# One more run of Strassen quads in the second half of each output projection

## The chip, the core and the metric

The kernel runs on one core of one Trainium2 chip. Five engines work in parallel, each through its own list of instructions in order: TensorE (PE in the profile, with its weight loads as PEld), VectorE (DVE), ScalarE (ACT), GpSimd (POOL) and SyncE (SP), which here only issues transfers. They wait for one another by semaphores. The metric is the device time of one execution in microseconds; lower is better. The kernel before takes 2047.71 us, the median of three runs that lie between 2047.55 and 2047.89.

## What is computed

A decoder trunk of two layers on 256 tokens of width 2048, all in float32. Layer 0 attends over one block, layer 1 over a window of 128 with shared keys and values; behind each attention stand an output projection, a residual with layer norm, a gated feed-forward net with a causal convolution of width 3, and a second residual with layer norm. Cut to the place that matters:

```python
h = x
for layer in range(2):
    attn = attention(h) @ w_o[layer]              # (256 x 2048) @ (2048 x 2048)
    h = layer_norm(ALPHA * h + attn, ln_g[layer, 0], ln_b[layer, 0])
    ffn = conv_ffn(h, w_up[layer], conv_w[layer], conv_b[layer], w_down[layer])
    h = layer_norm(ALPHA * h + ffn, ln_g[layer, 1], ln_b[layer, 1])
```

The change is in the two products with `w_o`.

## The kernel before, in words

**Numbers in two parts.** A float32 value is held as a high part in the fast format fp32r and a low part, the rest, in the same format. A product of two such matrices is three matmuls: high by high, high by low, low by high. `mm` and `product` issue these three (L497 to L499 for `product`). The high part of a weight tile is written by ACT (L168, `wh<-raw`), the low part by DVE (L177, `wl<-raw,wh`); `raw` is the tile as it was loaded.

**Halves.** Weights stream in as halves: tiles of 128 x 1024 float32, 512 KB, two blocks of 128 x 512 each. `load_weights` issues a load on SP as soon as the split of an older half frees one of 6 raw buffers; `split_upto` splits halves some places ahead of the one that PE takes. The split halves live in 4 buffers (`spool`), so that a split normally waits until PE has finished the half four places earlier. Near the end of a projection, `settle` gives some halves homes in tiles that are free by then (`xT`, the coming stage's `up`), and the table `reach` lets the splits run up to 9 halves ahead there.

**The output projection** (`project_out` with `PLAN_O`). Rows of the weight are 16 blocks of 128 (k), columns 4 chunks of 512 (n); the chunks are worked in two pairs, (0, 1) and (2, 3). A plain block (k, n) is multiplied with both groups of 128 tokens: two products, so a plain half is four. A quad is two rows k by the two chunks of a pair, by the two token groups: 8 products if plain, 7 by Strassen's scheme. `_mixed` writes the order: groups of plain halves, between them runs of two quads, each run 7 halves with two products each (`SEVEN`). Two of the seven halves (named T1,T3 and T2,T4) hold sums of weight blocks, which `presums` has made earlier on DVE (L444) and stored in DRAM; the sums of the token side are made by `sums` for each run, into xT, ahead of its first summed half.

**Banks.** A projection's partial results live in PSUM: four banks named acc, one for each chunk of a pair and group of tokens, and four named at, shared with the attention and the transposes. In a chunk pair with quads, the four at banks hold the shared products P1, P5, P7 and P6 through all runs of that pair. When the last run of the pair is over, `fold` adds them into the residual: three steps, put at the following three halves by `at`, of DVE instructions L513, L514, L518 (sums of the banks) and L612 or L614 (`into`: adds into `res`, the residual; the first time it also scales it by ALPHA; the last time L618 takes the statistics of the layer norm). `evac` does the same for an acc bank when its last product is done. A bank can be written anew when the last instruction that reads it has run.

**Order of the work.** The order on each engine is that in which the program issues its instructions (`manual_schedule`). `take` issues, for each half, the splits ahead and whatever `at` has put there; `step` counts the halves. Before: the first pair has 5 plain halves, 7 of a run, 3 plain, 7 of a run; the second pair 16 plain halves, the last 8 of which are the window, worked for the first group of tokens and then for the second, so that the layer norm of the first group runs under the second. 38 halves in all. In the window, `late` issues evacuations, the norm (L636, L637) and the transposes for the next stage (L670 on PE, from `res`).

Of the kernel before, what the change touches and what calls it, by code (L numbers as in the profile page):

```python
# [21 lines left out]
KB = D // P  # L22
NH = 16
# [4 lines left out]
NCH = D // 512  # L28
# [19 lines left out]
NQ = 12  # L48
PLAINS = ((5, 2, 2, 2, 2, 0, 6), (0, 1, 1, 1, 1, 0, 15))
NQ_O = 4  # L50
PLAINS_O = (5, 3, 0)
IN_PARTS = (True, False)
NV = 2 * 8 + 4 * 8
SEVEN = (("B11", "B21"), ("T1", "T3"), ("T2", "T4"), ("B22", "B22"), ("B11", "B21"), ("T1", "T3"), ("T2", "T4"))
# [10 lines left out]
def _mixed(c, groups, plain, p0):  # L65

    plan, at = [], 0
    for i, g in enumerate(groups):
        plan += plain[at:at + g]
        at += g  # L70
        if i < len(groups) - 1:
            plan += [tuple((b, p0 + 2 * i + p, c) for b, p in zip(bs, ps)) for bs, ps in zip(SEVEN, PAIR_OF)]
    assert at == len(plain)
    return plan


PLAN_O = _mixed(0, PLAINS_O, _plain(range(NH - 2 * NQ_O), (0, 1)), NH // 2 - NQ_O) + _plain(range(NH), (2, 3))
PLAN_V = _mixed(1, PLAINS_O, _plain(range(KB - 2 * NQ_O), (2, 3)), KB // 2 - NQ_O)
PLAN_DOWN = [h for c in range(2) for h in _mixed(c, PLAINS[c], _plain(range(2 * NQ, FT), (2 * c, 2 * c + 1)), 0)]
QUADS = {}  # L80
for _l in range(2):
    QUADS[2 * _l] = [(2 * _l, 0, NH // 2 - NQ_O + p) for p in range(NQ_O)]
    QUADS[2 * _l + 1] = [(2 * _l + 1, c, p) for c in range(2) for p in range(NQ)]
QUADS[4] = [(4, 1, KB // 2 - NQ_O + p) for p in range(NQ_O)]
ORDER = [q for li in (4, 0, 1, 2, 3) for q in QUADS[li]]
AHEAD_OF = {0: QUADS[4] + QUADS[0] + QUADS[1][:2], 1: QUADS[1][2:], 2: QUADS[2], 3: QUADS[3]}


def _summed(half):
# [17 lines left out]
def trunk(ctx: ExitStack, tc: tile.TileContext, wst, wsum, xT_in, x_in, relb, onehot, umask, sinks, conv_in, ln_g, ln_b, out):  # L107
# [449 lines left out]
    def project_out(src, plan, li, homes, preload, turnover=None, quad_blocks=None):  # L557
# [135 lines left out]

        def late(t, i):
            last = i == WINDOW - 1
            if t == 0 and last:
                evac(NCH - 1, 0)
                sd = moments(0)
                nc.vector.reciprocal(rs[0], sd)
                for c in COLS[0]:  # L700
                    norm(0, c)
            if t == 1 and after:
                if 3 <= i < 7:
                    c = COLS[0][i - 3]
                    low(0, c, turn(0, c))
                if 5 <= i < 7:
                    high_upto(n0 + i + 1)
            if t == 1 and last:
                evac(NCH - 1, 1)
                if after:  # L710
                    sd = moments(1)
                    nc.vector.reciprocal(rs[1], sd)
                else:
                    last_norm()
            if t == 1 and not after and 2 <= i < NCH + 1:
                scaled_ahead(i - 2)

        if quads:
            groups = PLAINS[0] if ns == 3 else PLAINS_O
            for i in range(len(groups) - 1):  # L720
                m = 4 if i and not groups[i] else sum(groups[:i]) + 7 * i - (ns == 3) if i else ns == 3
                for j, f in enumerate(sums(i)):
                    at(m + j, f)
        evacuated, folded = set(), set()
# [111 lines left out]
    def layer_attention(l, rest, stage, turnover):  # L836
# [65 lines left out]
        def v_pair():  # L902
            src = lambda k: xT[:, k, :]
            k0 = KB - 2 * NQ_O
            vts, begun = {}, set()

            def place(i):
                flat = st[:, NH // 2 + 4 * i:NH // 2 + 4 * i + 4, :].rearrange("p a b -> p (a b)")
                return flat.rearrange("p (h q s c) -> p h q s c", h=2, q=2, s=4)

            def into(t, n, a):
                if n not in vts:
                    vts[n] = pool.tile([P, 2, 512], F32, name="vt", bufs=2)
                d = vts[n][:, t, :]
                if (t, n) in begun:
                    nc.vector.tensor_tensor(out=d, in0=d, in1=a, op=ALU.add)
                else:
                    begun.add((t, n))
                    nc.scalar.activation(d, a, AF.Copy)

            parted = mixed(src, PLAN_V, k0 // 2, 4, lambda i: xT[:, k0 + 4 * i:k0 + 4 * i + 4, :], place, into)
            mv = Moving(src, 0)
            for i in range(len(PLAINS_O) - 1):
                for j, f in enumerate(parted.sums(i)):
                    at(sum(PLAINS_O[:i]) + 7 * i + j, f)
            evacuated = set()
            for half in PLAN_V:
                blocks = [mv.block() for _ in range(2)]
                for e, w in zip(half, blocks):
                    for tgt in parted.target(e):  # L930
                        parted.product(*tgt, *w)
                step()
                for n in (2, 3):
                    for t in range(2):
                        if (n, t) not in evacuated and parted.done((n, t)):
                            evacuated.add((n, t))
                            at(0, lambda n=n, t=t: into(t, n, parted.banks.pop((n, t))))
            parted.fold(1)
            run(before)
            return {n: in_parts(4 + i, v, "vt", 512, 2) for i, (n, v) in enumerate(sorted(vts.items()))}  # L940
# [280 lines left out]
```

## Time and profile before

| | us |
|---|---|
| median of 3 runs | 2047.71 |
| the profiled execution | 2047.9 |
| its span, first to last instruction | 2045.8 |
| PE busy in the span | 2035.9 |
| DVE busy | 1715.4 |
| ACT busy | 1159.0 |
| projection of layer 0 | about 294 to 385 |
| projection of layer 1 | about 1245 to 1335 |

The granted clock of TensorE is 1.00 over the whole span. The span is what the engines' instructions cover, and about 2 us of the execution lie around it. In a list in order of time, a row has start, duration, engine, line, operation, output<-inputs, and the number of equal instructions that it merges; in brackets stands how long the engine was idle before it and what ended this. A matmul's duration is its way through the array (0.39 us here), and the next starts before it ends, so the cost of a matmul is the distance between two starts.

### The profile page before, as it was taken

The numbers are of one execution on the slowest core, as the hardware profiler recorded it, in microseconds if no ns is written. First come the engines' busy times: TensorE is split into PE (matmuls) and PEld (weight loads), VectorE is DVE, ScalarE is ACT, GpSimd is POOL, SyncE is SP. The second block draws the span as 40 slices with busy tenths as digits, with TensorE's granted clock in tenths as the row PEclk, the third lists the DMA queues.
The fourth block names the chain that finished last, engine by engine and source line by source line (L and its number), as shares of the span: only waits on it lengthen the run. The fifth ranks groups of instructions, "written<-read, shape, count | busy, mean of one in ns | idle before, by whom it ended". The sixth has DMA issues, their size and how long they took to land.

```text
span 2045.8 us, 30050 instructions
## 1 busy us (share of the span) xinstructions
PE 2035.9 (100%) x10940; PEld 1760.4 (86%) x10940; DVE 1715.4 (84%) x2495; ACT 1159.0 (57%) x1737; POOL 79.6 (4%) x146
## 2 busy tenths in 40 slices
PE   9999999999999999999999999999999999999999
PEld 8888888988888888888888888898888888888887
DVE  6778888888888888899896788978888888889887
ACT  5556556455555555566673556545555555566673
POOL 0100000000000000000000000000000000000000
PEclk9999999999999999999999999999999999999999
DMA  8888888478888888889994767838888888879894
GB/s 299 307 293 320 286 297 303 167 249 302 283 296 295 288 295 290 286 282 330 330 364 156 263 214 251 288 126 291 307 300 312 305 300 302 299 265 328 314 357 165
DMA packets 161892, 578.19 MB, mean 283 GB/s; under 512 B 19360, under 2 KB 21728, under 8 KB 160464
## 3 DMA queue, kind: packets, MB, share of 16 engines
q1 hardware_dynamic: 138080, 500.08, 70.8%
q0 software_dynamic: 21312, 73.84, 9.2%
q10 hardware_dynamic: 2352, 2.36, 0.4%
q8 instruction: 86, 1.41, 0.3%
q14 instruction: 62, 0.51, 0.1%
HBM read 511.12 MB, written 69.26 MB: 284 GB/s over the span
## 4 chain that ended last, share of the span: by engine, by line
PE 93%; DVE 4%; issue 1%; DMA 1%; ACT 1%; DVEq 0%; ACTq 0%
PE acc L330 38%; PE acc L332 20%; PE acc L499 6%; PE acc L498 6%; PE acc L497 6%; PE at L498 2%; PE at L499 2%; PE at L497 2%; PE acc L357 1%; DVE wl L177 1%; DMA raw<-in_wst_dram 1%; PE acc L394 1%; PE acc L395 1%; PE acc L393 1%; PE acc L369 1%
## 5 line engine op out<-in xcount | busy, mean ns | idle before, releaser
L177 DVE TENSOR_TENSOR wl<-raw,wh 128x1024 fp32r<-128x1024 f32 (+1 forms) x760 | 905.5, 1220 | 160.7 <-ACT wh L168 138.3
L168 ACT ACTIVATE wh<-raw 128x1024 fp32r<-128x1024 f32 (+1 forms) x760 | 776.7, 1053 | 195.6 <-PE acc L499 113.2
L330 PE MATMUL acc<-xT,wh 128*128 128x512 f32 x3456 | 829.7, 392 | 0.0
L330 PEld LDWEIGHTS acc<-xT,wh 128*128 128x128 f32 x3456 | 642.5, 188 | 127.5
L332 PEld LDWEIGHTS acc<-xT,wl 128*128 128x128 f32 x3456 | 443.4, 190 | 11.9
L332 PE MATMUL acc<-xT,wl 128*128 128x256 f32 x3456 | 451.0, 284 | 0.0
L1035 ACT ACTIVATE h<-acc 128x256 f32<-128x256 f32 x172 | 66.0, 384 | 409.2 <-PE acc L332 203.4
L1043 DVE SCALAR_TENSOR_TENSOR c<-h,cw,c 128x255 f32<-128x255 f32 x344 | 165.4, 481 | 9.1 <-ACT c L1039 2.8
L444 DVE TENSOR_TENSOR gb<-gb 128x512 f32<-128x512 f32 x240 | 164.2, 684 | 0.0
L1036 DVE TENSOR_TENSOR h<-acc,h 128x256 f32<-128x256 f32 x172 | 72.5, 422 | 57.3 <-ACT h L1035 57.0
L448 POOL DMA_DIRECT2D ws<-gb x120 | 64.1, 534 | 1414.1 <-DVE gb L444 1122.1
L497 PE MATMUL acc<-wh,up 128*128 128x512 f32 x275 | 107.1, 390 | 0.0
L498 PE MATMUL acc<-wl,up 128*128 128x512 f32 x275 | 107.1, 390 | 0.0
L499 PE MATMUL acc<-wh,up 128*128 128x512 f32 x275 | 107.1, 389 | 0.0
L1039 ACT ACTIVATE c<-h,cw 128x256 f32<-128x256 f32 x172 | 101.9, 592 | 0.0
L497 PE MATMUL acc<-wh,st 128*128 128x512 f32 x178 | 70.1, 394 | 0.0
L499 PE MATMUL acc<-wh,st 128*128 128x512 f32 x178 | 69.4, 390 | 0.0
L498 PE MATMUL acc<-wl,st 128*128 128x512 f32 x178 | 69.4, 390 | 0.0
L497 PEld LDWEIGHTS acc<-wh,up 128*128 128x128 f32 x275 | 51.7, 188 | 10.7
L498 PEld LDWEIGHTS acc<-wl,up 128*128 128x128 f32 x275 | 51.7, 188 | 10.6
L499 PEld LDWEIGHTS acc<-wh,up 128*128 128x128 f32 x275 | 51.7, 188 | 10.6
L948 ACT ACTIVATE qT<-acc 128x256 f32<-128x256 f32 x32 | 12.3, 384 | 71.5 <-PE acc L332 46.1
(231 smaller groups left out, 2219.1 us busy)
## 6 DMA issues: line engine op xcount, KB each, us to landing
raw<-in_wst_dram SPq DMA_DIRECT2D x692, 512.0 KB, 5.2
gb<-in_wsum_dram SPq DMA_DIRECT2D x120, 512.0 KB, 7.7
ws<-gb POOLq DMA_DIRECT2D x120, 512.0 KB, 5.7
raw<-ws SPq DMA_DIRECT2D x120, 512.0 KB, 5.7
bias<-band POOLq DMA_DIRECT2D x8, 512.0 KB, 8.4
band<-ud POOLq DMA_DIRECT2D x4, 512.0 KB, 12.0
band<-ud ACTq DMA_DIRECT2D x4, 512.0 KB
res<-in_x_dram SPq DMA_DIRECT2D x2, 1024.0 KB, 7.3
```

Source lines behind the costliest of these rows:

```text
L168: nc.scalar.activation(wh[:, c], raws[s][:, c], AF.Copy)
L177: nc.vector.tensor_tensor(out=wl[:, c], in0=raws[s][:, c], in1=wh[:, c].bitcast(F32), op=ALU.subtract)
L330: nc.tensor.matmul(acc, w, xT[:, k, :], start=(k == 0), stop=(k == ends[0]))
L332: nc.tensor.matmul(acc[:, 0:T], w, xT[:, k, 0:T], start=False, stop=(k == ends[1]))
L444: nc.vector.tensor_tensor(out=w[:, o:o + 512], in0=a, in1=b, op=op)
L497: nc.tensor.matmul(acc, sh, wh, start=first, stop=False)
L498: nc.tensor.matmul(acc, sh, wl, start=False, stop=False)
L499: nc.tensor.matmul(acc, sl, wh, start=False, stop=last)
L1035: nc.scalar.activation(h, acc[:, T:2 * T], AF.Copy)
L1036: nc.vector.tensor_tensor(out=h, in0=acc[:, 0:T], in1=h, op=ALU.add)
L1039: nc.scalar.activation(c, h, AF.Identity, bias=w[:, 3:4], scale=w[:, 2:3])
L1043: nc.vector.scalar_tensor_tensor(c[:, d:T], h[:, 0:T - d], w[:, 2 - d:3 - d], c[:, d:T], op0=ALU.mult, op1=ALU.add)
```

## The change

The first chunk pair keeps its two runs, with 4, 2 and 2 plain halves around them where there were 5, 3 and 0. The second pair begins with a run of two quads (rows 12 to 15 of the weight), and 12 plain halves follow. Its token-side sums are those that the second run of the first pair has made already. Per projection 41 halves then stand where there were 38. The sums of weight blocks for these quads are two more per layer: those of layer 0 are made in the first attention stage, in place of two of the down projection's, which move into the feed-forward stage together with layer 1's two. `late` evacuates acc banks that become complete within the window. The last hunk only keeps the value projection, which shared the table, at 5, 3, 0.

```diff
-PLAINS_O = (5, 3, 0)
+PLAINS_O = (4, 2, 2)
+PLAINS_V = (5, 3, 0)
...
-PLAN_O = _mixed(0, PLAINS_O, _plain(range(NH - 2 * NQ_O), (0, 1)), NH // 2 - NQ_O) + _plain(range(NH), (2, 3))
-PLAN_V = _mixed(1, PLAINS_O, _plain(range(KB - 2 * NQ_O), (2, 3)), KB // 2 - NQ_O)
+PLAN_O = _mixed(0, PLAINS_O, _plain(range(NH - 2 * NQ_O), (0, 1)), NH // 2 - NQ_O) + _mixed(
+    1, (0, 12), _plain(range(NH - NQ_O), (2, 3)), NH // 2 - 2)
+PLAN_V = _mixed(1, PLAINS_V, _plain(range(KB - 2 * NQ_O), (2, 3)), KB // 2 - NQ_O)
...
-    QUADS[2 * _l] = [(2 * _l, 0, NH // 2 - NQ_O + p) for p in range(NQ_O)]
+    QUADS[2 * _l] = [(2 * _l, c, NH // 2 - NQ_O + p) for c in range(2) for p in range(2 * c, NQ_O)]
...
-AHEAD_OF = {0: QUADS[4] + QUADS[0] + QUADS[1][:2], 1: QUADS[1][2:], 2: QUADS[2], 3: QUADS[3]}
+AHEAD_OF = {0: QUADS[4] + QUADS[0], 1: QUADS[1] + QUADS[2][:2], 2: QUADS[2][2:], 3: QUADS[3]}
...
         def late(t, i):
             last = i == WINDOW - 1
+            for n in range(NCH - 1):
+                if (n, t) not in evacuated and done((n, t)):
+                    evacuated.add((n, t))
+                    evac(n, t)
...
-                m = 4 if i and not groups[i] else sum(groups[:i]) + 7 * i - (ns == 3) if i else ns == 3
+                m = 4 if i and not groups[i] else sum(groups[:i]) + 7 * i - (groups[i] == 2) if i else ns == 3
```

In the changed kernel all lines of the projection stand a few lines lower (L497 is L499, L612 is L614, L614 is L616, L618 is L620, L177 is L179).

**PE, end of the first chunk pair, layer 0.** Of each product the first of its three matmuls is shown. Before, behind the last run (its last three products are the first three rows), the plain halves of the second pair follow on acc banks:

```order
L497 MATMUL at_3371<-xT_143 128x512
L497 MATMUL at_3381<-xT_143 128x512 [waits Activation_49]
L497 MATMUL acc_3212<-xT_143,st_145 128x512
L497 MATMUL acc_3609<-xT_143,st_145 128x512 [waits Activation_49]
L497 MATMUL acc_3613<-xT_143,st_145 128x512
L497 MATMUL acc_3609<-xT_143,st_145 128x512
L497 MATMUL acc_3613<-xT_143,st_145 128x512
```

Now, from the last product of the two plain halves behind the run (first row), the new run follows, with new at banks, and its first matmuls carry waits for DVE:

```order
L499 MATMUL acc_3446<-wh_3536,st_149 128x512
L499 MATMUL at_3613<-wh_3549,st_149 128x512 [waits Activation_49]
L499 MATMUL acc_3617<-wh_3549,st_149 128x512
L499 MATMUL at_3630<-xT_147 128x512 [waits DVE_49]
L499 MATMUL at_3634<-xT_147 128x512 [waits DVE_49]
L499 MATMUL at_3648<-xT_147 128x512 [waits DVE_49,Activation_49]
L499 MATMUL acc_3652<-xT_147,st_149 128x512
```

What moved: at_3630, at_3634 and at_3648 are the new P5, P7 and P6, written two plain halves and one or two run halves behind the old run's end. By the semaphore counts of the built program, the wait of the at_3634 row is met by DVE's L520 from at_3348 (the old P7), and that of the at_3648 row by DVE's L614 from at_3344 (the old P5). Before, no at bank was written there until the transposes of the window.

**DVE, the fold of the first pair, layer 0.** Before, the last rows of the fold (at_3367 is the P5 bank; no one waits for it):

```order
L618 BN_STATS stats_3188<-res_144 128x6
L518 TENSOR_TENSOR tmp_3595<-at_3371,tmp_3595 128x512
L177 TENSOR_TENSOR xT_143<-raw_3571,xT_143 128x1024
L177 TENSOR_TENSOR xT_143<-raw_3581,xT_143 128x1024
L612 TENSOR_TENSOR res_144<-res_144,tmp_3595 128x512
L618 BN_STATS stats_3188<-res_144 128x6
L612 TENSOR_TENSOR res_144<-res_144,tmp_3595 128x512
L612 TENSOR_TENSOR res_144<-res_144,at_3367 128x512
```

Now the fold begins with these rows (acc_3216 is an acc bank, at_3365 the P6 bank):

```order
L179 TENSOR_TENSOR wl_3550<-raw_3480,wh_3549 128x1024
L616 SCALAR_TENSOR_TENSOR res_148<-res_148,acc_3216 128x512
L179 TENSOR_TENSOR xT_147<-raw_3492,xT_147 128x1024
L614 TENSOR_TENSOR res_148<-res_148,tmp_3561 128x512
L620 BN_STATS stats_3192<-res_148 128x6
L515 TENSOR_TENSOR tmp_3561<-at_3365,tmp_3561 128x512
L516 TENSOR_TENSOR tmp_3561<-at_3344,tmp_3561 128x512
```

and goes on, without a row left out, to the one for which the at_3648 row above waits:

```order
L179 TENSOR_TENSOR xT_147<-raw_3504,xT_147 128x1024
L616 SCALAR_TENSOR_TENSOR res_148<-res_148,tmp_3561 128x512
L520 TENSOR_TENSOR tmp_3561<-at_3348,tmp_3561 128x512
L614 TENSOR_TENSOR res_148<-res_148,acc_3378 128x512
L620 BN_STATS stats_3192<-res_148 128x6
L616 SCALAR_TENSOR_TENSOR res_148<-res_148,acc_3446 128x512
L179 TENSOR_TENSOR xT_147<-raw_3516,xT_147 128x1024
L179 TENSOR_TENSOR up_3413<-raw_3528,up_3413 128x1024
L614 TENSOR_TENSOR res_148<-res_148,tmp_3561 128x512
L620 BN_STATS stats_3192<-res_148 128x6
L614 TENSOR_TENSOR res_148<-res_148,tmp_3561 128x512
L614 TENSOR_TENSOR res_148<-res_148,at_3344 128x512
```

What moved: the evacuations of acc_3378 and acc_3446, banks of the chunk whose plain halves now end two halves behind the run, stand inside the fold, fewer splits do, and PE stands behind the last row.

**PE, start of the first run, layer 0.** Before, with the last head's attention (at_3354 is its output bank, L766 to L817), two products stand between it and the row that waits for DVE, which is the first on P6:

```order
L766 MATMUL at_3354<-PTh_3184,vth_2074 128x256 [waits Activation_49]
L767 MATMUL at_3354<-PTl_3185,vth_2074 128x256 [waits DVE_49]
L817 MATMUL at_3354<-PTr_3186,vt_1984 128x128 [waits Activation_49]
L497 MATMUL at_3367<-wh_3289,xT_143 128x512
L497 MATMUL at_3371<-wh_3289,xT_143 128x512 [waits PE_49]
L497 MATMUL at_3381<-wh_3314,xT_143 128x512 [waits DVE_49]
L497 MATMUL acc_3212<-wh_3314,st_145 128x512
```

Now P6 follows that attention directly, and waits for the same DVE row, the one that empties the output bank (at_3352):

```order
L499 MATMUL at_3348<-wh_3267,xT_147 128x512
L772 MATMUL at_3352<-PTh_3188,vth_2078 128x256 [waits DVE_49]
L773 MATMUL at_3352<-PTl_3189,vth_2078 128x256
L823 MATMUL at_3352<-PTr_3190,vt_1988 128x128
L499 MATMUL at_3365<-wh_3293,xT_147 128x512 [waits DVE_49]
L499 MATMUL acc_3216<-wh_3293,st_149 128x512
```

What moved: the run begins one half earlier, the attention's steps stand where they stood, and so P5 and P7 come ahead of them.

More of the change, by code (lines that the diff above doesn't have):

```diff
@@ L922, in v_pair @@
             mv = Moving(src, 0)
-            for i in range(len(PLAINS_O) - 1):
+            for i in range(len(PLAINS_V) - 1):
                 for j, f in enumerate(parted.sums(i)):
-                    at(sum(PLAINS_O[:i]) + 7 * i + j, f)
+                    at(sum(PLAINS_V[:i]) + 7 * i + j, f)
             evacuated = set()
```

## The prediction

> **What bounds the kernel now.** I read first the page's busy times, then who waited for whom on PE, then the busy time by stage, and last the two projections row by row.
>
> ```profile
> PE 2035.9 (100%) x10940; PEld 1760.4 (86%) x10940; DVE 1715.4 (84%) x2495; ACT 1159.0 (57%) x1737; POOL 79.6 (4%) x146
> ...
> PE at L767 <- DVE PTl L808: 2.1, 3, 0.9
> ...
> PE at L670 <- DVE res L637: 0.2, 1, 0.2
> ...
> 331.60:373.50 41.90, 41.90 (x186) 34.74 (x185) 41.62 (x47) 26.99 (x28) 0.00 (x0) 1.00 0.81 294
> ...
> 385.00:860.00 475.00, 475.00 (x2794) 422.26 (x2794) 396.02 (x613) 258.38 (x422) 22.38 (x42) 1.00 0.80 277
> ```
>
> PE is the bound: no wait of it is longer than 0.9 us once the kernel has started. In the rows by stage the columns are the stretch, its length, then busy time of PE, PEld, DVE, ACT and POOL, granted clock, DMA share and GB/s. They say two things. In the feed-forward stage (385 to 860) DVE is free for 79 us. In the second half of the projection (331.6 to 373.5) it is not: 41.62 of 41.90 us. There PE runs without a gap only because the splits are up to 9 halves ahead and because nothing on PE needs what else DVE does in these 42 us. So matmuls saved count in full only while PE needs nothing from DVE early.
>
> **What is removed.** A product is three matmuls.
>
> ```profile
> 337.97 0.39 PE L499 MATMUL at<-xT 128*128 128x512 f32 x1
> 338.20 0.39 PE L497 MATMUL acc<-xT,st 128*128 128x512 f32 x1
> 338.42 0.39 PE L498 MATMUL acc<-xT,st 128*128 128x512 f32 x1
> 338.65 0.39 PE L499 MATMUL acc<-xT,st 128*128 128x512 f32 x1
> 338.88 0.39 PE L497 MATMUL acc<-xT,st 128*128 128x512 f32 x1
> ```
>
> From 338.20 to 338.88 a product takes 0.68 us; a plain half is four (2.72), a run's half two (1.36). Two quads save two products: **-1.36 us per layer**, 2.7 us in all. The first row also is the end of the last run of the first pair, 338.2.
>
> **The new bank wait, the largest term.** P5, P7 and P6 of the new run take banks that the fold of the first pair must have read. Before, the fold's end looks like this, with the prices:
>
> ```profile
> L168 ACT ACTIVATE wh<-raw 128x1024 fp32r<-128x1024 f32 (+1 forms) x760 | 776.7, 1053 | 195.6 <-PE acc L499 113.2
> ...
> 332.12 0.68 DVE L614 SCALAR_TENSOR_TENSOR res<-res,acc 128x512 f32<-128x512 f32 x1
> ...
> 351.56 2.35 DVE L177 TENSOR_TENSOR xT<-raw,xT 128x1024 fp32r<-128x1024 f32 x2
> 353.83 0.69 DVE L612 TENSOR_TENSOR res<-res,tmp 128x512 f32<-128x512 f32 x1
> 354.55 0.69 DVE L618 BATCH_NORM_STATS2 stats<-res 128x6 f32<-128x512 f32 x1
> 355.16 0.67 DVE L612 TENSOR_TENSOR res<-res,tmp 128x512 f32<-128x512 f32 x1
> 355.87 0.69 DVE L612 TENSOR_TENSOR res<-res,at 128x512 f32<-128x512 f32 x1
> ...
> 371.20 2.35 DVE L177 TENSOR_TENSOR up<-raw,up 128x1024 fp32r<-128x1024 f32 x2
> 373.47 0.68 DVE L614 SCALAR_TENSOR_TENSOR res<-res,acc 128x512 f32<-128x512 f32 x1
> ```
>
> Two splits take 2.27 us (351.56 to 353.83), one 1.135. From 332.12 to 373.47 DVE runs 25 splits and 20 other operations of 128x512 without a gap: 41.35 - 28.4 = 13.0, so one of these takes 0.65. The P5 bank is read at 355.87 to 356.56, 18.4 us after the run's end. Nobody waits for it.
>
> Now count from the end of that run in the changed order. PE has two plain halves (5.44 us) and two halves of the new run (2.72) until its first product on P6, which needs the bank of the old P5: due at 8.16. DVE: ACT writes the high part for the split `wl_3537` once PE has left that buffer, two run halves before the run's end, so ACT ends at -2.72 + 0.16 + 1.06 = -1.5; that split (1.14 from -1.4) and an evacuation (0.6) follow, and the row `wl_3550<-raw_3480`, the first one shown in the changed order, starts at +0.3. From it to the L614 that frees the old P5 stand 19 rows, 5 splits and 14 others: 5.7 + 9.2 = 14.9, end at 15.2. With 0.1 for the semaphore PE goes on at 15.3: **+7.1 us per layer**, some 0.8 of it already at P7. Below, the wait can't be under 3.0: the third row after P7's, the evacuation of acc_3446, waits for PE's last plain product (5.44 + 0.16), and with it 2 splits and 5 others are left (5.5), end at 11.1. Above, I take the 18.4 us of before: 10.2. I take the count, since both its prices and the saturation it supposes are in these rows. Queued behind the waiting matmul is the rest of the run and all plain halves, everything in PE's order.
>
> The nearest place where the program reuses these banks is the down projection:
>
> ```profile
> 972.68 0.69 DVE L612 TENSOR_TENSOR res<-res,at 128x512 f32<-128x512 f32 x1
> ...
> 975.69 0.39 PE L497 MATMUL at<-wh,st 128*128 128x512 f32 x1
> ```
>
> Six plain halves, 16.3 us, lie between there; the read ends 2.3 us before the next write. With two plain halves that margin is gone.
>
> **At the start of the first run** (both layers) P6 now directly follows the last head's output, whose bank it takes. The wait is for ACT and DVE to empty it:
>
> ```profile
> 312.44 0.39 PE L767 MATMUL at<-PTl,vth 128*128 128x256 f32 x1 [0.94 <-DVE PTl L808]
> ...
> 312.78 0.38 PE L817 MATMUL at<-PTr,vt 128*128 128x128 f32 x2
> ...
> 313.20 0.38 ACT L824 ACTIVATE st<-at 128x256 fp32r<-128x256 f32 x1 [0.69 <-PE at L817]
> ...
> 313.69 0.42 DVE L825 TENSOR_TENSOR st<-at,st 128x256 fp32r<-128x256 f32 x1
> ...
> 314.39 0.39 PE L497 MATMUL at<-wh,xT 128*128 128x512 f32 x1
> ...
> 1261.87 0.38 PE L820 MATMUL at<-PT,vt 128*128 128x128 f32 x2
> ...
> 1263.92 0.42 DVE L825 TENSOR_TENSOR st<-at,st 128x256 fp32r<-128x256 f32 x1
> ```
>
> In layer 0 the bank is free at 314.1, 0.95 us after the output's end (313.16); P6 came at 314.39 and waited for nothing. In layer 1 it took 2.1 us (1262.25 to 1264.34), since a split stood ahead on DVE. **+1.1 us per layer**, bounds 0.9 and 2.1. The wait of 0.94 at L767 stays, as the attention's chain is as late with a shorter half ahead of it; I add 0.2 per layer for it (0 to 1.3). The second run's token sums get one half's less lead: +0.1.
>
> **The window.** DVE gains 3 splits and 8 fold operations per layer (8.6 us), PE loses 1.36. Once PE has waited 7 us, they are level again: from 15.1 on, 20 splits and 11 others are 29.9, so the evacuation that starts the norm comes at 45.0; PE ends the first group of tokens at 15.3 + 5 x 1.36 + 4 x 2.72 + 10.88 = 43.9. So it is 1.1 late, 2.1 if the loads slip, where it is now 1.95:
>
> ```profile
> 371.52 0.39 PE L497 MATMUL acc<-xT,st 128*128 128x512 f32 x1
> ...
> 377.23 0.66 PE L670 MATMUL at<-ident,res 128*128 128x128 f32 x4
> ...
> raw<-in_wst_dram SPq DMA_DIRECT2D x692, 512.0 KB, 5.2
> ```
>
> 371.52 is the first matmul of the second group, 1.95 before the 373.47 above; the transpose at 377.23 pays 0.1 for it. Term: 0, bounds -0.2 and +1. A load needs 5.2 us and 6 buffers turn at 1.135, which is why it may slip. Costed at nothing: 16 more L444 operations in the first feed-forward stage, about 10 us under DVE's 79 free ones, and their 8 loads and 8 stores; with no cover it would be up to 10 us, but PE has no gap in that stage.
>
> **The pace after the wait.** A gap of 6 us occurs nowhere in this trace. Behind the 0.94 above PE goes on at full pace. At its start it does not:
>
> ```profile
> 1.36 4.10 PE L275 MATMUL at<-ident 128*128 128x128 f32 x18 [1.36 <-POOL ident masks.py:199]
> 5.36 0.79 PE L393 MATMUL acc<-wh,xT 128*128 128x512 f32 x1
> ...
> 6.74 0.39 PE L393 MATMUL acc<-wh,xT 128*128 128x512 f32 x1
> 6.97 0.39 PE L394 MATMUL acc<-wl,xT 128*128 128x512 f32 x1
> ```
>
> Three matmuls take 1.38 us from 5.36 to 6.74, 0.46 each, against 0.23 from 6.74 to 6.97: half pace, until 5.4 us after the first transpose, though the granted clock stands at 1.00. Bounds: 0 (as after 0.94) and half of 5.4, 2.7. Neither row is near, so I take the middle, **+1.3 per layer**. The Trainium skill, "TensorE: Matmul & The Clock Gate", Part 1, speaks against the change here: it says that PE falls to half clock after an idle window of about 3.4 us and returns after about as long a busy one. The start agrees with that (0.46 against 0.23); no row here shows it in mid-kernel. By that rule the term is an estimated 1.7 (half of 3.4) or more, and the sum 2065.3 or more.
>
> **Sum.** Per layer -1.36 + 7.1 + 1.1 + 0.2 + 0.1 + 0 + 1.3 = 8.4; two layers 16.9. The profiled execution (2045.8 span, 2047.9 in all) goes to 2064.8, the median of 2047.71, 0.2 lower, to **2064.5 us**, 0.8% slower.
>
> **Rivals.** (1) *The saving arrives, not slower*: DVE reads the old banks within 8.2 us of the run's end, and P6 of the first run finds its bank free; 2047.7 - 2.7 = 2045.0. For it: PE has no such waits now. Against it: DVE has no idle time there, and even an idle DVE leaves 3.0. It decides from a bank wait under about 1.3 us per layer on. Chance 0.03. (2) *DVE is ahead of my count*, as the reads come with the lower bound: 2 x (-1.36 + 3.0 + 0.9 + 0.1) = 5.3, and no loss of pace in a gap that short: 2053. Against it: 41.62 of 41.90. Chance 0.12. (3) *DVE is later*, as in before's own 18.4 us, because raw loads slip: 2 x 3.1 more, 2070.7; for it, the 5.2 us loads. Chance 0.12. (4) *The lost time shows at the turn too*, with the norm 3 us later than counted in each layer: 2070.5. Chance 0.08. My own, the bank wait with the pace term anywhere between its bounds, 2061.9 to 2067.3: 0.64, and 0.01 for a gain that I don't see. The range of 8 in 10 is 2056 to 2071: its lower end lies between (2) and mine, its upper end takes in most of (3) and (4). A measurement can tell 0.2% (4.1 us) from no change, and (1) would be no change: slower 0.95, same 0.04, faster 0.01.
>
> **What would show it.** In the changed profile: two waits of PE of 5 to 7 us with matmuls onto at of L499 as waiters and DVE's `res<-res,at` (L614) as releaser, one per layer, about 8 us after the first pair's last run; a shorter one before them for L520; one of about 1 us for the st rows of L831 (L825 before). DVE busy without a gap from there to the norm. Matmuls 0.43 to 0.46 apart behind the wait if the pace falls. It is wrong if PE's longest wait in the projections stays under 2 us, or if the time lies in another stage.

## The result, and the profile after

The changed kernel takes 2066.94 us (median of 5 runs, 2065.86 to 2068.76) against 2047.71 (5 runs, 2047.33 to 2047.89): a ratio of 1.0096 with a 95% interval of 1.0085 to 1.0106, slower. The prediction was 2064.5 in a range of 2056 to 2071. The profiled execution is one of 2066.94 us with a span of 2065.2, so the spans differ by 19.4 us (2045.8 before). Of these, 9.98 lie ahead of the first matmul of layer 0's feed-forward stage. The two rows below are that matmul, in order of time, in the kernel before and then in the changed one:

```profile
384.60 4.00 PE L357 MATMUL acc<-xT,wh 128*128 128x256 f32 x32
```

```profile
394.58 1.59 PE L359 MATMUL acc<-xT,wh 128*128 128x256 f32 x12
```

The same matmul of layer 1, before and now:

```profile
1335.08 4.00 PE L357 MATMUL acc<-xT,wh 128*128 128x256 f32 x32
```

```profile
1354.22 3.99 PE L359 MATMUL acc<-xT,wh 128*128 128x256 f32 x32
```

It is 19.14 us later, so 9.16 us belong to layer 1, and 0.3 us of the 19.4 come after it. The waits of PE in the changed kernel (engine, line, releaser; then us in total, times, longest):

```profile
PE at L499 <- DVE res L614: 11.9, 2, 6.0
PE at L499 <- DVE st L831: 1.6, 2, 0.9
...
PE at L499 <- DVE tmp L520: 1.3, 2, 0.7
```

The first row is the bank of the old P5, the third that of the old P7, the second the output bank of the last head. No row for the turn (L670, 0.2 before) is among them. The place itself, in order of time, PE and DVE with rows left out; the first is the plain product behind the old run's last:

```profile
335.12 0.39 PE L499 MATMUL acc<-wh,st 128*128 128x512 f32 x1
...
344.00 0.40 PE L501 MATMUL at<-xT 128*128 128x512 f32 x1
...
348.80 0.67 DVE L614 TENSOR_TENSOR res<-res,tmp 128x512 f32<-128x512 f32 x1
349.50 0.69 DVE L614 TENSOR_TENSOR res<-res,at 128x512 f32<-128x512 f32 x1
...
350.33 0.77 PE L499 MATMUL at<-xT 128*128 128x512 f32 x1 [5.93 <-DVE res L614]
...
350.90 0.63 PE L500 MATMUL at<-xT 128*128 128x512 f32 x1
...
351.33 0.63 PE L501 MATMUL at<-xT 128*128 128x512 f32 x1
```

DVE reads the old P5 from 349.50 to 350.19, and PE starts on that bank 0.14 us later. Behind the wait the matmuls stand 0.43 us apart. The windows around it say why; the third number from the end is the granted clock (stretch, length, busy PE, PEld, DVE, ACT, POOL, clock, DMA share, GB/s):

```profile
344.40:350.33 5.93, 0.00 (x0) 0.03 (x1) 5.83 (x9) 1.89 (x3) 0.00 (x0) 0.64 0.53 151
350.33:356.00 5.67, 5.67 (x13) 4.43 (x14) 5.67 (x6) 2.15 (x3) 0.00 (x0) 0.50 0.60 198
356.00:358.00 2.00, 2.00 (x9) 1.64 (x8) 2.00 (x3) 0.68 (x2) 0.00 (x0) 0.93 1.00 360
...
1304.50:1310.40 5.90, 0.00 (x1) 0.00 (x0) 5.80 (x9) 1.62 (x3) 0.00 (x0) 0.85 0.52 162
1310.40:1314.00 3.60, 3.55 (x8) 2.81 (x9) 3.60 (x4) 1.64 (x2) 0.00 (x0) 0.50 0.41 131
1314.00:1316.00 2.00, 2.00 (x7) 1.62 (x6) 2.00 (x3) 0.57 (x1) 0.00 (x0) 0.64 0.92 252
```

At half clock half of the time is lost: 5.67 x 0.50 + 2.00 x 0.07 = 3.0 us in layer 0, 3.60 x 0.50 + 2.00 x 0.36 = 2.5 us in layer 1.

So far the profile reads as a bill of PE's waits. The first product on the new P6 was due 8.16 us after the run's end, at 335.12 + 8.16 = 343.28, and starts at 350.33, 7.05 late (two gaps of 0.67 and 5.93, and the slow restart behind each). Layer 0 has -1.36 (two products, not seen alone) + 7.05 + 1.06 (gaps of 1.07 and 0.93 at the first run, where one of 0.94 stood before) + 3.0 (pace) = 9.75 of 9.98 us. Layer 1, with bank gaps of the same length, has -1.36 + 7.05 + 0.63 + 2.5 = 8.8 of 9.16. The remaining 0.9 us in all are not assigned. Whether these waits are also the cause is another question, and the runs answer it differently.

### The profile page after: what moved, and what is told of

Same layout as the page of the kernel before. It is cut to its first block, busy times and chain, and to the rows that moved or that the text cites. A ratio compares the mean times of both kernels' runs of the same rounds, so it can differ in the third digit from the quotient of the medians.

```text
span 2065.2 us, 30167 instructions
## 1 busy us (share of the span) xinstructions
PE 2040.3 (99%) x10928; PEld 1759.5 (85%) x10928; DVE 1741.8 (84%) x2533; ACT 1166.9 (57%) x1745; POOL 84.1 (4%) x154
## 4 chain that ended last, share of the span: by engine, by line
PE 95%; DVE 2%; DMA 1%; issue 1%; ACT 1%; DVEq 0%; ACTq 0%
PE acc L332 38%; PE acc L334 20%; PE acc L499 7%; PE acc L500 7%; PE acc L501 7%; PE at L499 3%; PE at L501 3%; PE at L500 3%; PE acc L359 1%; PE acc L396 1%; PE acc L397 1%; PE acc L395 1%; DVE wl L179 1%; PE acc L371 1%; DMA raw<-in_wst_dram 1%
## 5 line engine op out<-in xcount | busy, mean ns | idle before, releaser
L179 DVE TENSOR_TENSOR wl<-raw,wh 128x1024 fp32r<-128x1024 f32 (+1 forms) x766 | 912.0, 1219 | 158.1 <-ACT wh L170 136.5
L446 DVE TENSOR_TENSOR gb<-gb 128x512 f32<-128x512 f32 x256 | 175.3, 685 | 0.1
L450 POOL DMA_DIRECT2D ws<-gb x128 | 68.5, 535 | 1430.1 <-DVE gb L446 1285.7
L499 PE MATMUL acc<-wh,up 128*128 128x512 f32 x275 | 107.0, 389 | 0.0
L499 PE MATMUL acc<-wh,st 128*128 128x512 f32 x182 | 71.5, 393 | 0.0
L499 PEld LDWEIGHTS acc<-wh,up 128*128 128x128 f32 x275 | 51.6, 188 | 10.7
```

The lines of the kernel that those rows point to most:

```text
L179: nc.vector.tensor_tensor(out=wl[:, c], in0=raws[s][:, c], in1=wh[:, c].bitcast(F32), op=ALU.subtract)
L446: nc.vector.tensor_tensor(out=w[:, o:o + 512], in0=a, in1=b, op=op)
L450: nc.gpsimd.dma_start(wsums[q][:, js], w[:, js])
L499: nc.tensor.matmul(acc, sh, wh, start=first, stop=False)
```

## The experiments

Theory A is the account of the prediction: PE waits for a bank, so what shortens that wait shortens the time. The first two runs take the change apart, the third and the next two shorten the wait, and from there on theory C stands against A.

### The two parts alone

The first kernel keeps the new dealing and leaves out the new run:

```diff
-    1, (0, 12), _plain(range(NH - NQ_O), (2, 3)), NH // 2 - 2)
+    1, (16,), _plain(range(NH), (2, 3)), 0)
...
```

> The dealing 4, 2, 2 alone, the second chunk pair plain as before (38 halves, and the quad sums made where they were). Theory A (the loss is PE's wait for the banks of the fold, with the slower pace behind it): nothing reuses the at banks behind the first pair, so only the wait for the last head's output bank at the start of the first run is left, about 1.1 us in layer 0 (with 0.2 at L772) and 0.6 in layer 1; 2047.7 + 1.9 = 2049.6. Rival (the dealing itself costs a good part of the 19 us): 2055 or more.

Measured: 2051.58 us (10 runs, 2049.86 to 2051.90), 1.0015 of before (1.0005 to 1.0025). PE waits for the last head as in the changed kernel (1.07 and 0.93 in layer 0, 0.64 in layer 1), and for no bank. Three of the ten executions took 2049.9 to 2050.1, the others 2051.4 to 2051.9. The profiled one, of 2051.62, shows what the 1.7 us between them may be, in the window behind the two short waits:

```profile
314.00:316.00 2.00, 2.00 (x7) 1.54 (x6) 0.00 (x0) 0.21 (x1) 0.00 (x0) 0.50 0.98 344
```

The clock fell to half here, behind two gaps of 1.07 and 0.93 us, though in the changed kernel's profile the same two gaps left it at 1.00. The mean clock of the whole execution agrees: 1.000 in the three short ones, 0.999 in the seven others. So the dealing costs 2 us by its waits, and another 1.7 when the clock falls. The second kernel keeps the old dealing and adds the run, so that no plain half lies between the old run and the new one:

```diff
-PLAINS_O = (4, 2, 2)
+PLAINS_O = (5, 3, 0)
```

> The new run alone, with the first pair left at 5, 3, 0. The new run then stands directly behind the last run of the first pair, so its first product on the old P5 bank is due 2.7 us behind that run's end, not 8.2. Theory A (PE stands behind the fold's reads, whose time goes by DVE's order): the read comes about 15 us behind the run's end, wait about 12 us per layer, in place of 6.6, and no wait for the last head's bank; per layer -1.4 + 12 + 2.6 of slower pace, 2074. Rival B (DVE's sum of work sets the end of the stage, wherever PE waits): as the changed kernel, 2066 to 2068.

Measured: 2074.63 us (2073.43 to 2075.19), 1.0129 (1.0114 to 1.0145), 7.7 us above the changed kernel. Its waits:

```profile
PE at L499 <- DVE res L614: 6.5, 2, 3.3
PE at L499 <- DVE tmp L520: 5.6, 2, 2.8
PE at L499 <- ACT tmp L513: 5.2, 2, 2.8
PE at L499 <- DVE tmp L515: 3.4, 2, 2.5
```

All four banks are waited for in turn, in the order in which the fold reads them: 20.7 us in all, where the changed kernel waits 13.2 for two. The new run carries the loss, and the two plain halves between the runs save 7.5 us of waiting. Rival B in its plain form, by which DVE's sum of work alone sets the end wherever PE waits (2066 to 2068), falls here. So far A holds.

### The banks read first

If A holds, the wait can be taken away by reading the two banks early. This kernel moves the instructions on P7 and P5 from the second and third step of the first pair's fold into its first step, ahead of splits and evacuations:

```diff
                 nc.vector.tensor_tensor(out=v, in0=p5, in1=u, op=ALU.add)
+                if early:
+                    nc.vector.tensor_tensor(out=u, in0=p7, in1=u, op=ALU.add)
+                    into(1, n1, p5)
...
```

> The changed kernel, in the fold of the first pair alone the two remaining bank reads (P7 and P5) come in its first step, right behind the read of P6; no instruction more or less. The bank wait falls from 6.6 us to under 1.5. Theory A (the order of the reads is the bound): the wait and the slower pace go, 2 x (6 + 2.6) less, about 2050. Rival B (DVE has no time for this work in that stretch): the splits come as late as now, the evacuation that starts the norm can move from 382.0 to about 380.5 at best, so PE waits about 6 us at the first transpose of the window instead: 2061.5, or up to 2067 if the pace falls there too.

Measured: 2067.31 us (2066.07 to 2070.28), 1.0097 (1.0082 to 1.0112). The waits for the banks are gone, and nothing is won. The waits of PE:

```profile
PE at L677 <- DVE res L644: 6.8, 2, 3.7
PE acc L500 <- DVE xT L179: 3.8, 2, 1.9
PE at L499 <- DVE st L836: 1.6, 2, 0.9
```

The first row is the turn: the transposes wait for the norm. The second is a split that now stands behind the early reads. Theory A falls here; it had expected 2050. Rival B had the place right, but had expected 6 us of waiting there.

Theory C takes its place: **two ends of nearly the same date bound the second half of the projection. One is PE's wait for the bank, set by the order of DVE's work. The other is the norm of the first group of tokens, set by the amount of DVE's work ahead of it.** Shortening one shows the other.

### The bank wanted later

The next two kernels leave the order of the reads and put one or two plain halves between the old run and the new one, so that the bank is due 2.7 or 5.4 us later; the splits of one or two halves are let in a little earlier for it. The diff is that with one half; with two it is (2, 10), and `reach[w0 - 3]` is set as well.

```diff
-    1, (0, 12), _plain(range(NH - NQ_O), (2, 3)), NH // 2 - 2)
+    1, (1, 11), _plain(range(NH - NQ_O), (2, 3)), NH // 2 - 2)
...
+            if ns == 4:
+                reach[w0 - 4] = w0 + 3
```

> The changed kernel with the second pair dealt (1, 11): one plain half of weights stands between the two runs, so that the product P6 of the new run wants its bank one half, some 2.7 us, later (the loads of one half are let in a little earlier, so that no buffer deadlock arises). By the count that the prediction used, the bank is free at the same date, so the wait falls from 5.9 to some 3.2 us a layer; if nothing else set the end, the time were 2066.9 - 2 x 2.7 - 2 x 1 (less half pace) = 2059.5, down to 2057. Theory C: VectorE's whole work is the same and was only 0.8 us early at the turn, so that what is won at the bank shows again as a wait at the turn: 2063 to 2067.

> As the run with one plain half between the two runs, with two of them: the bank is wanted 5.4 us later, and the wait falls to 0.5 us or nothing. By the bank alone: 2066.9 - 2 x 5.9 - 2 x 2.7 (no half pace) = 2050, up to 2053. Theory C: the wait moves to the turn whole, as with the early reads: 2062 to 2067, with 1.5 to 4 us a layer waited for the norm.

Measured: 2065.38 us (2064.41 to 2066.57), 1.0085 (1.0070 to 1.0100), with one half; 2066.03 (2063.77 to 2068.61), 1.0090 (1.0073 to 1.0107), with two. The waits with one half:

```profile
PE at L499 <- DVE res L616: 8.3, 2, 4.2
PE at L674 <- DVE res L641: 4.2, 2, 2.8
```

and with two, where the profile names no releaser for two of the groups:

```profile
PE at L674 <- issue: 4.9, 1, 4.9
PE at L674 <- DVE res L641: 3.9, 1, 3.9
PE at L499 <- issue: 2.8, 2, 1.4
```

The wait at the bank (L499) falls from 13.2 us (two rows in the changed kernel) to 8.3 and 2.8, and the wait at the turn (L674) rises from nothing to 4.2 and 8.8: 13.2, 12.5 and 11.6 together. The wait wanders from the one place to the other, and the time stays within 1.6 us. By the bank alone it had to come down to 2059.5 and 2050.

The date that does not move is DVE's. The row in which DVE closes the first group's statistics (layer 0), before, with the early reads, with one half between, and with two:

```profile
374.92 0.26 DVE L625 BATCH_NORM_AGGREGATE ag<-stats 128x2 f32<-128x24 f32 x1
```

```profile
383.61 0.26 DVE L632 BATCH_NORM_AGGREGATE ag<-stats 128x2 f32<-128x24 f32 x1
```

```profile
383.52 0.26 DVE L629 BATCH_NORM_AGGREGATE ag<-stats 128x2 f32<-128x24 f32 x1
```

```profile
383.61 0.26 DVE L629 BATCH_NORM_AGGREGATE ag<-stats 128x2 f32<-128x24 f32 x1
```

It is 8.6 or 8.7 us later than before in three arrangements that differ by up to 5.4 us in when the bank is wanted. In the changed kernel itself it stands at 383.47, and 0.83 us of that is DVE waiting for PE. The prediction had counted the work that the change adds to DVE in this stretch: 3 splits and 8 operations of the fold, 8.6 us. That the two figures agree so closely is in part luck. With the dealing alone, which gives DVE no operation more ahead of this row, it already is 1.65 us later:

```profile
376.57 0.26 DVE L627 BATCH_NORM_AGGREGATE ag<-stats 128x2 f32<-128x24 f32 x1
```

The run adds the other 7.0, and in the three arrangements 1.5 to 1.7 us ahead of the row are DVE waiting for ACT, where before it waits for nothing from 331 us on.

### Less work for DVE, with and without the bank wait

If C holds, taking work from DVE helps only where the bank wait is gone. Both kernels leave out the fold of the second pair's run (8 DVE instructions a layer), the first in the kernel with the early reads, the second in the changed kernel as it is:

```diff
+        folds = paired if ns == 3 else {0}
...
                     folded.add(c)
-                    fold(c)
+                    if c in folds:
+                        fold(c)
```

> This is the kernel with the early reads of banks P7 and P5, and beside it the new run's fold is left out in both layers (three additions of the products' sums and five additions into the rows, 8 VectorE instructions of 0.7 us a layer, so that the second chunk pair's columns lack their quad part): VectorE gets some 5.3 us less work between the new run's end and the turn. Theory C: two ends of nearly the same date bound a changed projection, the bank that the old run's last read frees (through the order of VectorE's work) and VectorE's whole work up to the first norm (through its amount); the early reads took the first away, so that the second showed as waits of 3.7 and 3.1 us at the turn. Less work on VectorE then ends these two waits, with half-clock time of some 1 to 2 us a layer behind them: 2067.3 - 6.8 - 3 = 2057, between 2054 and 2061, with the waits on the split of weights (1.9 us a layer) left. Rival D: the turn's wait comes from weights that arrive late (loads released later), not from VectorE's amount of work: no less than 2064.

> The changed kernel, with the banks read in its own order, and the same 8 VectorE instructions a layer left out (the new run's fold; the second chunk pair's columns lack their quad part). They stand behind the bank wait and ahead of the turn. Theory C: the bank waits of 5.9 us and the half pace behind them stay, and VectorE is already 0.8 us early for the turn, so that nothing is won: 2065 to 2068, as the changed kernel. If VectorE's amount of work alone set the end: 2067 - 2 x 5.3 = 2056 to 2058.

Measured with early reads: 2059.74 us (2058.91 to 2060.78), 1.0058 (1.0043 to 1.0073), 7.6 us less than the same kernel with the fold. Its longest waits and DVE's closing row:

```profile
PE acc L500 <- DVE xT L179: 3.8, 2, 1.9
PE at L500 <- DVE up L179: 2.2, 2, 1.9
...
380.51 0.27 DVE L633 BATCH_NORM_AGGREGATE ag<-stats 128x2 f32<-128x24 f32 x1
```

No wait at the turn is left in layer 0, and 0.2 us in layer 1. The date comes 3.1 us earlier, not 5.3, in part because DVE then waits for ACT in between (2.8 us in four waits, 1.5 in two with the fold). The weights were not late by themselves, so rival D (no less than 2064) is out. What is left are waits for splits, 6.0 us in the two rows above, so the two ends of C are not the only ones. Measured with the bank wait in place: 2066.78 us (2066.29 to 2068.72), 1.0094 (1.0079 to 1.0109), as the changed kernel. Its first wait:

```profile
PE at L499 <- DVE res L615: 11.9, 2, 6.0
```

and the row of DVE that starts the norm, the last evacuation:

```profile
382.00 0.69 DVE L617 SCALAR_TENSOR_TENSOR res<-res,acc 128x512 f32<-128x512 f32 x1 [2.92 <-PE acc L501]
```

DVE now waits 2.92 us here for PE, where it waited 0.83 in the changed kernel: the relief turns into idle time of DVE. The four kernels cross the two causes: 2066.94 (late reads, all work), 2067.31 (early reads, all work), 2066.78 (late reads, less work) and 2059.74 (early reads, less work). Neither step alone wins anything; the second, behind the first, wins 7.6 us. Both expectations of C are met, and that is the test on which I rest it.

### The array kept busy

The pace has its own run: 26 additional matmuls on a spare bank stand ahead of the waiting P6 in each projection, so that PE is busy through the wait. They add work and change no result.

```diff
...
+            if ns == 4 and i == 24:
+                banks[2, 1] = psum.tile([P, 512], F32, name="acc")
+                used[2, 1] = 0
+                for _ in range(26):
+                    nc.tensor.matmul(banks[2, 1], src(0)[:, 0:P], blocks[0][0], start=True, stop=True)
```

> The changed kernel with 26 matmuls of 128x512 per projection ahead of the first product on P6, into an acc bank that is free and is begun anew afterwards, so that PE is busy for 5.9 us of the wait. The wait's end does not move (350.3 in layer 0). If the half pace behind the wait (0.43 us between matmuls) is the clock that falls when PE is idle, it is gone: 0.23 us from the first matmul on, 2.8 and 2.4 us less, of which the norm chain on DVE, only about 0.8 us early, takes some back at the first transpose: 2062 to 2063. If the pace has another cause (loads, ports), it stays and the time is 2066 to 2068.

Measured: 2065.01 us (2063.67 to 2065.76), 1.0083 (1.0068 to 1.0098). Behind the wait, clock and waits:

```profile
350.78:356.00 5.22, 5.22 (x23) 4.35 (x24) 5.22 (x6) 1.67 (x3) 0.00 (x0) 1.00 0.55 178
...
PE at L673 <- DVE res L640: 1.8, 2, 1.1
```

The granted clock stays at 1.00 where it was 0.50, with 23 matmuls in 5.22 us where 13 took 5.67: the pace after a wait is the clock's doing. It was worth 5.5 us on PE (3.0 + 2.5), but the time falls by 1.9 only, short of the 2062 to 2063 expected. 1.8 us come back as a wait at the turn, which is C again: PE's slow pace was hidden in part behind DVE. The other 1.8 us are not assigned.

### DVE's work given to GpSimd

A version that would beat both kernels needs DVE relieved without leaving anything out. GpSimd has nothing to compute there. 8 splits of weights a layer move to it, in the kernel with the early reads and, as a control, in the kernel before:

```diff
-        nc.vector.tensor_tensor(out=wl[:, c], in0=raws[s][:, c], in1=wh[:, c].bitcast(F32), op=ALU.subtract)
+        eng = nc.gpsimd if s in beside else nc.vector
+        eng.tensor_tensor(out=wl[:, c], in0=raws[s][:, c], in1=wh[:, c].bitcast(F32), op=ALU.subtract)
...
+            if ns == 4:
+                beside.update([w0 + j for j in (1, 3, 4, 7)] + [n0 + 4 + j for j in range(len(following))])
```

> The kernel with the early reads, all of its arithmetic there, and 8 low-half splits a layer (those of weight halves ahead of the window and of the FFN's first, 1.22 us each on VectorE) moved to GpSimd, which has nothing else to compute there: VectorE gets 8 x 1.13 = 9 us a layer less. Theory C: the waits at the turn (3.7 and 3.1) end and the one on the split of weights shrinks; what is left are the short waits at the run's start (2.0 and 0.6 us) against 2.7 us of products saved: 2047 to 2055. It is open how long GpSimd takes for a split, since no row shows one: if it takes over some 6 us, or slows VectorE beside it, the splits come late and the time is above 2060. Rival D (late loads): no less than 2064.

> The kernel before with the same 8 splits a layer on GpSimd, and nothing else changed. In its profile the chain of waits runs through VectorE from 330 to 384 us while TensorE waits nowhere, so that VectorE and TensorE end level: theory C expects no gain from less work on VectorE alone, 2046 to 2048; a loss would be GpSimd's own price, and is to be taken from the run before it.

Measured: 2077.09 us (2075.20 to 2078.30), 1.0141 (1.0126 to 1.0157), and 2050.91 (2050.50 to 2053.96), 1.0017 (1.0008 to 1.0027). Both are misses: C had expected 2047 to 2055 and 2046 to 2048, with the proviso for the first that GpSimd could be slow or slow DVE down. In order of time, from the first of the two (with the early reads):

```profile
368.47 5.26 DVE L180 TENSOR_TENSOR up<-raw,up 128x1024 fp32r<-128x1024 f32 x2
369.50 3.14 POOL L180 TENSOR_TENSOR up<-raw,up 128x1024 fp32r<-128x1024 f32 x1 [0.20 <-ACT up L170]
...
376.90 9.03 DVE L180 TENSOR_TENSOR wl<-raw,wh 128x1024 fp32r<-128x1024 f32 x4
378.12 6.72 POOL L180 TENSOR_TENSOR up<-raw,up 128x1024 fp32r<-128x1024 f32 x2 [5.47 <-DVE wl L180]
```

and from the second (the kernel before with the splits moved):

```profile
348.65 2.41 POOL L178 TENSOR_TENSOR xT<-raw,xT 128x1024 fp32r<-128x1024 f32 x1 [34.41 <-ACT xT L168]
348.74 3.40 DVE L178 TENSOR_TENSOR wl<-raw,wh 128x1024 fp32r<-128x1024 f32 x1
351.32 3.07 POOL L178 TENSOR_TENSOR up<-raw,up 128x1024 fp32r<-128x1024 f32 x1 [0.27 <-ACT up L168]
352.06 2.88 DVE L615 TENSOR_TENSOR res<-res,tmp 128x512 f32<-128x512 f32 x1
...
375.87 2.75 DVE L640 SCALAR_TENSOR_TENSOR res<-res,rs,gb 128x512 f32<-128x512 f32 x1
```

A split takes GpSimd 2.4 us or more against DVE's 1.22, and while it runs DVE's operation stands still: the split that began at 348.74 takes 3.40 us and ends at 352.14, 1.08 after GpSimd's at 351.06; four splits from 376.90 take 9.03 us where four take 4.62 elsewhere. DVE lost more than it gave away: in the first kernel PE's wait at the turn grew to 13.5 us in total (longest 7.9), in part because DVE there waits 3.9 us for ACT ahead of layer 0's norm, in place of 1.5. In the second the last row is an operation of layer 0's norm, which takes 0.75 us elsewhere; in layer 1 a split of 3.42 us stands ahead of the norm. PE then waits 1.3 us for the norm in each layer, 2.6 of the 3.0 us. The Trainium skill, "SBUF — State Buffer", section "SBUF: two separate sides", states this: a DVE operation with two inputs in SBUF and a GpSimd operation that reads SBUF hold one pair of ports in turn, and the second stands still until the first is done. The rows agree. So both times measure mainly this lock, and they neither bear out C nor speak against it. How fast the changed order would be with DVE truly relieved stays open; no version that beats the kernel before was found.

## Why the prediction came out

The time was 2.4 us above the forecast and well inside the range. By its steps:

- **The bank wait**, +7.1 per layer, from a read that ends 15.2 us after the run's end and a product due at 8.16. Measured: the read ends at 15.1 (350.19 against 335.12), and PE is 7.05 late. The prices of 1.135 for a split and 0.65 for the others held, and so did the count of 19 rows. (In the kernel before I had taken the run's end one product too early, at 338.2 in place of 338.9; what rested on it are the upper bound and the price of the third rival, each 0.7 too high per layer.)
- **The start of the first run**, +1.1 and 0.2: 1.06 in layer 0, 0.63 in layer 1. The split that stood ahead on DVE in layer 1 before was not in the way. Too high by 0.2 and 0.7.
- **The token sums**, +0.1: no wait for them is seen.
- **The turn**, 0 with bounds -0.2 and +1, from DVE at 45.0 and PE at 43.9 after the run's end. No wait is there in the changed kernel, so the term is right as a sum, and by the run with the array kept busy for a reason that I had not seen: at full pace PE waits 1.1 us in layer 0 and 0.6 in layer 1. That nothing is paid there is luck. In the changed kernel PE is late by its half clock, and DVE waits for it:

```profile
382.02 0.69 DVE L614 TENSOR_TENSOR res<-res,acc 128x512 f32<-128x512 f32 x1 [0.83 <-PE acc L501]
```

- **The pace**, +1.3, the middle of 0 and 2.7: measured 3.0 and 2.5. This is the term that was mis-sized. The end of the bounds that the kernel's own start gave was the right one, and layer 0 went a little past it. The Trainium skill's rule ("TensorE: Matmul & The Clock Gate", Part 1), by which the sum was 2065.3 or more, was nearer than my middle.
- **The sums of weight blocks**, costed at nothing: from the first matmul of layer 0's feed-forward stage to P6's wait at the start of layer 1's first run the changed kernel takes 878.46 us (394.58 to 1273.04), and the dealing alone, without these operations, 878.48 (387.39 to 1265.87). Right.

Per layer the sum was 8.4, and 9.75 and 8.8 are found in its place: the pace adds 1.7 and 1.2, the start of the run takes 0.2 and 0.7, the token sums 0.1. Part of the nearness is that these errors have opposite signs.

What the prediction did not see is how its terms hang together. It says that PE bounds the kernel and that the bank wait is the largest term. Both hold: with the bank wait in place, 8 operations less on DVE win nothing (2066.78), and with the bank wanted earlier the time rises (2074.63). But it had also written down what makes a second bound: DVE full for 41.62 of 41.90 us, 8.6 us of work added to it per layer, and both engines level at the turn. So the bank wait could be taken away without winning anything, which no sentence of the prediction says; the runs with the early reads and with the later bank show it. The prediction's fourth rival, the loss at the turn *in addition* to the bank, was wrong for the same reason: the two waits stand in for one another (13.2, 12.5 and 11.6 us together).

The chain of waits of the kernel before pointed there. In layer 0, from 335 to 377 us, where PE has no gap, it runs through DVE and not through PE; its shares by line in that window:

```profile
by line: DVE up L177 18.9%; issue 16.2%; DVE xT L177 15.7%; DMA raw<-in_wst_dram 13.6%; DVE wl L177 13.2%; DVE res L612 7.5%; DVE stats L618 5.2%; DVE res L614 4.3%; DVE res L636 1.8%; DVE res L637 1.8%; DVE tmp L518 1.6%; DVE tmp L513 1.4%
```

The prediction rests on busy times, waits and windows of that stretch, and not on the chain in it. The chain says only that DVE ends last, by the 0.1 us that the transposes pay; how much a change there costs, it does not say.

Of the rivals, *the saving arrives* and *DVE is ahead of my count* fall with the 5.9 us at the bank; *DVE is later* falls with 15.1 against 15.2.

## What to carry to other kernels

Before saving time on the busiest engine, ask in the same stretch which engine the chain of waits runs through. Where a second engine is full and ends level with the first, two bounds of nearly the same date stand side by side, and the wait that the profile shows is only the one that ends last. Test it by removing that wait: if the time stays and another wait of the same size appears, there is a second bound. Then take work from the engine that both waits name, once with the first wait removed and once with it kept; if only the first of these wins, both bounds are real. Before giving such work to an idle engine, measure whether the two can run side by side: here they could not.

## What had not been expected of the hardware

The clock falls after much shorter gaps than 6 us, and not always. Two gaps of 1.07 and 0.93 us within 2.9 us brought it to 0.50 for some 3 us in one profiled execution (the dealing alone), and left it at 1.00 in the changed kernel's. A single gap of 1.89 us did so in the kernel with the early reads, some 1.3 us after PE had gone on, and not in the same kernel with the second fold left out, where it fell only behind the next gap, of 1.90 us (0.50 from 353.00 to 356.00). The window behind the first gap, in the one kernel and in the other:

```profile
347.35:350.30 2.95, 2.95 (x10) 2.35 (x11) 2.92 (x4) 0.54 (x1) 0.00 (x0) 0.73 0.58 192
```

```profile
347.35:350.30 2.95, 2.95 (x12) 2.17 (x12) 2.92 (x4) 0.67 (x1) 0.00 (x0) 1.00 0.57 185
```

In the gap of 5.93 us the mean clock of 0.64 means that it fell some 1.7 us after PE's last matmul (0.28 of the gap at full, the rest at half), in layer 1's gap of 5.95 us some 4 us after (0.85). A count that begins with the gap would not give two dates so far apart. One over fixed stretches of time, whose phase differs from run to run, would; no run tests this. The Trainium skill ("TensorE: Matmul & The Clock Gate", Part 1) has such free-running windows, of about 3.4 us, but its table of the two states lets the clock fall after an idle one. No gap of 0.9 to 1.9 us can fill such a window, so here the measurement decides. The times of such a kernel scatter with the clock: 2.9 us between the lowest and the highest of 5 runs, against 0.6 before, with a mean clock of 0.997 in the shortest and 0.994 in the longest.

A GpSimd operation on SBUF and a DVE operation with two SBUF inputs did not overlap in the rows shown: the one held the other for its whole length (3.40 us for a split of 1.22). DVE operations with one input in PSUM kept their time beside GpSimd: in the kernel before with the splits moved, the L519 at 355.59 takes 0.67 us while a GpSimd split runs from 354.35 to 357.22, and the L617 at 372.92 takes 0.68 while two run from 372.12 to 378.07.
